# Differential attention: the softmax reciprocal used in place, a shorter output norm, and new operation times in the planner

## The chip, the core and the metric

The kernel runs on one core of a Trainium2 chip. The metric is device time in microseconds (us) of one launch. The core's engines are TensorE (PE; its weight loads are listed as PEld), VectorE (DVE), ScalarE (ACT) and GpSimd (POOL); SyncE (SP) issues the DMAs. Each engine works through its own instructions in their order, and engines wait for each other by semaphores.

## What is computed

One decoder layer: three token mixers (a convolution branch, differential attention, cross-attention into memory), each projected and gated, summed, and projected once more. The change lies in differential attention: 8 heads over 1024 positions, two causal softmax maps each, and an RMS norm of each head's output.

```python
s = einsum(q, k) * scale + bias            # bias = -slope_h * distance, causal
p = softmax(s)                             # two maps, m = 0 and 1
a = p[:, :, 0] - lam * p[:, :, 1]
o = einsum(a, v)
o = rms_norm(o, subln_g) * (1.0 - lambda_init)
o = o * silu(gate) ; y_diff = o @ w_proj
```

## The kernel before

All is float32; matrix products that need precision are split into a high and a low half, three matmuls for one. The kernel has stages. Ahead of attention come the input projections and the convolution. The attention stage comes next, and behind it the last projections (the second half of the attention projection with a GH/GL operand, heads 4 to 7, then the output projection).

**A group of attention** is one head and 256 queries (`g`, two blocks `t` of 128): 32 groups, heads in order, and within a head `g` in the order 2, 3, 0, 1. A group's steps are:

- `pair` (`scores`): for one block and up to 512 keys, four matmuls write two `sc` banks (L1032, L1034). DVE adds the distance bias out of the bank and takes the row maximum (L1038). When a block has all its keys, DVE makes `nm` (L1050), ACT takes the two exponentials with their sums (L1052), DVE makes the reciprocals `rc` (L1054) and a factor (L1055) and combines both maps into one (L1056). POOL copies the first map's reciprocal into a tile `r0` (L1058), since the block's rows are divided by it only in the norm.
- `trans`: PE turns four 128x128 blocks of the combined map into a `tp` bank (L1076), ACT copies it out as `a` (L1078).
- `prod`: PE multiplies `a` with the values into the bank `av` (L1084). After a group's last one, ACT copies `o` out (L1089) and `norm` is issued.
- `norm`: ACT squares `o * r0` with a sum per row (L1098); `rstd_of` makes 1/sqrt from Ln and Exp on ACT (L174, L175) and one Newton step of five POOL operations (L173, L176 to L179); POOL multiplies by `r0` (L1101), DVE scales `o` (L1103).
- `turned`, below called the o-turn: PE turns `o` (L1110), ACT scales it by the norm's gain (L1113), POOL multiplies the gate (L1114), and SP stores it (L1116 for heads 4 to 7).

**Filler.** Projections that need nothing of the running group are cut into steps of six 128x512 matmuls (L78, L79, L80 with operands hH/hL). There are 136 such steps from the first score matmul on; 104 belong to two earlier branches, 32 to the projection of heads 0 to 3, which may start only when the o-turn of head 3's last group is placed.

**What sets the order.** PE's order is written by a planner that runs when the kernel is built. It keeps a clock `now` and lists of the times when DVE, ACT and POOL are busy; `run(eng, start, *costs)` books operations there (each cost times `SLACK`, 1.25, plus `HOP`, 0.3). Of the streams load, prod, trans, pair and o-turn it takes the step that is ready first; when the best one is not ready within `IDLE` (0.4) of `now`, it places a filler step instead, while there are any:

```python
if used < len(fill) and free and best[0] > max(now, fill_at) + IDLE:
    ...
    f()
    used += 1
```

The numbers in `pair_step`, `prod_step`, `trans_step` and so on are this planner's durations in us. They set no time on the chip, but decide which step stands next on PE. The other engines' order is made by a scheduler from the program with PE's order given. What is left of the filler when the streams are empty runs behind the attention stage, while the last o-turns go out to memory and come back as the operand `gin` (L1365) of the next stage.

Of the kernel before, what the change touches and what calls it, by code (L numbers as in the profile page):

```python
# [15 lines left out]
P = 128  # L16
# [14 lines left out]
def hybrid_layer(  # L31
# [36 lines left out]
    def new(pool, shape, tag, dt=F32, bufs=None):  # L68
        return pool.tile(shape, dt, tag=tag, name=tag, bufs=bufs)
# [896 lines left out]
    with ExitStack() as st:  # L966
# [42 lines left out]
        def scores(h, g, T, A):  # L1009

            slope = 2.0 ** -(h + 1)
            A["p"], A["r0"] = [], None
            steps = []
            for t in range(2):
                i = 2 * g + t
                n = P * (i + 1)
                nh = (n + 511) // 512
                R = {}
                for hf in range(nh):
                    def pair(t=t, i=i, n=n, hf=hf, nh=nh, R=R):  # L1020
                        if t == 0 and hf == 0:
                            A["r0"] = new(tiny, [P, 2], "r0", bufs=4)
                        if hf == 0:
                            R["mx"] = new(tiny, [P, 2, 2], "mx")
                            R["p"] = (new(ap_, [P, (2 * g + 2) * P], f"p{g}"), new(ap_, [P, S], "p"))
                        mx, pm = R["mx"], R["p"]
                        k0 = hf * 512
                        w = min(512, n - k0)
                        sc = [mm_bank("sc") for _ in range(2)]
                        q, ts = T["q", i // 4], slice(i % 4 * P, i % 4 * P + P)  # L1030
                        for m in range(2):
                            nc.tensor.matmul(sc[m][:, :w], lhsT=q[:, m, ts], rhs=T["k", hf][:, m, :w],  # L1032
                                             start=True, stop=False)
                            nc.tensor.matmul(sc[m][:, :w], lhsT=q[:, m, ts], rhs=T["kL", hf][:, m, :w],  # L1034
                                             start=False, stop=True)
                        d0 = S - P - P * i + k0
                        for m in range(2):
                            nc.vector.tensor_tensor_reduce(  # L1038
                                out=pm[m][:, k0:k0 + w], in0=sc[m][:, :w], in1=dist[:, d0:d0 + w], scale=1.0,
                                scalar=-3.0e38, op0=ALU.add, op1=ALU.max, accum_out=mx[:, hf, m:m + 1])  # L1040
                        if hf < nh - 1:
                            return
                        p0, p1 = pm
                        nm = new(tiny, [P, 2], "nm")
                        sm = new(tiny, [P, 2], "sm")
                        rc = new(tiny, [P, 2], "rc")
                        c1 = new(tiny, [P, 1], "c1")
                        if nh == 2:
                            nc.vector.tensor_tensor(mx[:, 0, :], mx[:, 0, :], mx[:, 1, :], op=ALU.max)
                        nc.vector.tensor_scalar_mul(nm, mx[:, 0, :], -slope)  # L1050
                        for m in range(2):
                            nc.scalar.activation(pm[m][:, :n], pm[m][:, :n], AF.Exp, bias=nm[:, m:m + 1],  # L1052
                                                 scale=slope, accum_out=sm[:, m:m + 1])
                        nc.vector.reciprocal(rc, sm)  # L1054
                        nc.vector.tensor_scalar(c1, sm[:, 0:1], rc[:, 1:2], nlam[:, 0:1], op0=ALU.mult, op1=ALU.mult)  # L1055
                        nc.vector.scalar_tensor_tensor(p0[:, :n], p1[:, :n], c1[:, 0:1], p0[:, :n],  # L1056
                                                 op0=ALU.mult, op1=ALU.add)
                        nc.gpsimd.tensor_copy(A["r0"][:, t:t + 1], rc[:, 0:1])  # L1058
                        A["p"].append(p0)
                    steps.append(pair)  # L1060
            return steps

# [30 lines left out]

        def norm(A):
            o, ss, y = A["o"], new(tiny, [P, 2], "oss"), new(tiny, [P, 2], "osy")
            junk = new(ap_, [P, P], "ojunk", bufs=1)
            for t in range(2):
                nc.scalar.activation(junk, o[:, t * P:(t + 1) * P], AF.Square, scale=A["r0"][:, t:t + 1],  # L1098
                                     accum_out=ss[:, t:t + 1])
            rstd_of(y, ss, [P, 2], 1.0 / P, 1e-6, eps6, pool=tiny, tags=("onv", "ont"))  # L1100
            nc.gpsimd.tensor_tensor(y, y, A["r0"], op=ALU.mult)  # L1101
            for t in range(2):
                nc.vector.tensor_scalar_mul(o[:, t * P:(t + 1) * P], o[:, t * P:(t + 1) * P], y[:, t:t + 1])  # L1103

        def turned(h, g, A):

# [15 lines left out]
                nc.sync.dma_start(dst[h][:, sl], r2f(src))  # L1122

        ORDER, IDLE = (2, 3, 0, 1), 0.4
        PARTS, SLACK, HOP, CHAIN, LOAD, AB, CHUNK, FIRST = 4, 1.25, 0.3, 8.0, 3.0, 3, 3.0, 11.0

        def bank(W, b, r, c0, half, done, parts):

# [68 lines left out]
        for n, steps in enumerate(todo):  # L1197
            if n == 29:
                held = len(fill)
            fill += [(f, 0.0, False) for at, f in ahead_of if at == n]  # L1200
            (begin, first), *more = steps

            ahead = todo[n + 1][0][0] if n + 1 < len(todo) else lambda: None
            begins[len(fill)] = begin
            steps = [lambda f=first, ahead=ahead: (ahead(), f())] + more
            fill += [(f, UNIT, f is steps[-1]) for f in steps]
# [11 lines left out]
        def run(eng, start, *costs):  # L1218

            for c in costs:  # L1220
                c, q = c * SLACK, busy[eng]
                at = next((i for i in range(len(q)) if q[i][1] > start and max(q[i - 1][1] if i else 0.0, start) + c
                           <= q[i][0]), len(q))
                start = max(q[at - 1][1] if at else 0.0, start)
                q.insert(at, (start, start + c))
                del q[:-40]
                start += c
            return start + HOP
# [5 lines left out]
        def el(n):  # L1234
            return 0.06 + n / 960

        def pair_step(n, h, g, t, hf, f):
            i = 2 * g + t
            w, last_ = min(512, P * (i + 1) - hf * 512), (i + 1) * P <= hf * 512 + 512
            needs = [("cut", h, i // 4), ("cut", h, hf)] + ([("turned", n - 4)] if hf == 0 and n >= 4 else [])  # L1240

            def after(at):
                for m in range(2):
                    x = run("DVE", at - 2 * w / 2400 * (1 - m) + HOP, el(w))
                    slots.append(x)
                    slots.pop(0)
                if last_:
                    t_of["read", h, g] = at
                    w_ = P * (i + 1)
                    x = run("DVE", x, 0.07, 0.07) if hf else run("DVE", x, 0.07)  # L1250
                    x = run("ACT", x, *[0.1 + el(w_)] * 2)
                    x = run("DVE", x, 0.08, 0.19)
                    x = run("DVE", x, el(w_))
                    t_of["p", n, t] = x
            return f, needs, lambda: max(slots[0], now + ahead() - AHEAD), 4 * w / 2400, after

# [12 lines left out]
        def prod_step(n, h, g, jp, c, f):  # L1269
            def after(at):  # L1270
                t_of["used", c] = at
                if jp == g:
                    t_of["av", n] = run("ACT", at + HOP, 0.27)
                    t_of["o", n] = run("DVE", run("ACT", t_of["av", n], 0.17, 0.17) + CHAIN, 0.17, 0.17)
                    t_of["done", h, g] = at
            needs = [("a", c), ("turn", h, jp // 2)] + ([("av", n - 1)] if n else []) + \
                    ([("norm2", n - 4)] if jp == g and n > 3 else [])
            return f, needs, lambda: 0.0, 4 * (384 if jp == g else 512) / 2400, after
# [48 lines left out]
        while any(streams.values()):  # L1327
# [8 lines left out]
            if used < len(fill) and free and best[0] > max(now, fill_at) + IDLE:  # L1336
                now = max(now, fill_at)
                f, cost, end = fill[used]
                with tc.high_priority(offset=0 if cost else -60):
                    f()  # L1340
                used += 1
                now += cost
                parts += cost > 0
                if end:
                    run("DVE", now + HOP, el(512))
                    fill_at = now + CHUNK if parts in chunks else 0.0
                continue
# [89 lines left out]
```

## Time and profile before

| | us |
|---|---|
| median of 3 runs (lowest, highest) | 1762.25 (1761.45, 1763.59) |
| profiled execution | 1759.21 |
| its span | 1757.4 |
| PE busy | 1653.6 |
| DVE, ACT, POOL busy | 1294.1, 919.6, 910.3 |
| attention stage, first score matmul to first matmul on GH | 1212.0 to 1617.0 |

The span is the time from the first to the last instruction of the profiled execution; 1.8 us lie around it. Matmuls are pipelined, so a row's PE time overlaps the next row's: the pace of PE is read from the starts of successive matmuls. A line's idle time is what the engine stood still ahead of it, with the instruction that ended the wait. The granted clock is 1.00 for 2.4 GHz and 0.50 for 1.2 GHz.

### The profile page before, as it was taken

To read this page: it belongs to the slowest core of one execution; us is meant where nothing else is said; L and a number is where in the kernel's file an instruction comes from. 1 tells how busy PE (TensorE), PEld (TensorE's weight loads), DVE (VectorE), ACT (ScalarE), POOL (GpSimd) and SP (SyncE) were. 2 spreads that over 40 slices of the span, in tenths; PEclk is the share of its full clock that TensorE was granted. 3 is DMA by queue.
4 is the path that set the end of the run, shared out by engine and by line. 5 is a ranking of instruction groups with operands and counts; after the bars stand their busy time and mean duration, and the time that the engine had idled before them with its cause. 6 is when DMAs were issued, how large, how long until landed. Compare 5 with 4: busy or idle time off the path is not lost. (4 is left out here: it accounts for less than half of the span.)

```text
span 1757.4 us, 24237 instructions
## 1 busy us (share of the span) xinstructions
PE 1653.6 (94%) x7882; PEld 1369.1 (78%) x7882; DVE 1294.1 (74%) x2170; ACT 919.6 (52%) x1949; POOL 910.3 (52%) x921
## 2 busy tenths in 40 slices
PE   6999999989999999888999999989997999999999
PEld 5788888868787777667888778867786878877787
DVE  7879997998999999675764797744665676675911
ACT  5614635334444445465655786753666776763300
POOL 3320201688765666555665676545547564557820
PEclk8999999999999999999999999999998999999999
DMA  7410212232333345543444233278577455565632
GB/s 273 147 33 19 90 50 76 96 112 86 118 110 95 114 139 162 174 162 120 150 162 151 85 97 121 77 276 253 152 236 259 125 174 159 151 225 189 212 115 90
DMA packets 201399, 247.51 MB, mean 141 GB/s; under 512 B 15377, under 2 KB 109590, under 8 KB 201272
## 3 DMA queue, kind: packets, MB, share of 16 engines
q1 hardware_dynamic: 201272, 245.96, 43.5%
q8 instruction: 62, 1.02, 0.2%
q14 instruction: 65, 0.53, 0.1%
HBM read 172.50 MB, written 73.40 MB: 140 GB/s over the span
## 5 line engine op out<-in xcount | busy, mean ns | idle before, releaser
L422 DVE SCALAR_TENSOR_TENSOR cv<-u,cw,cv 128x512 f32<-128x512 f32 x464 | 349.0, 752 | 9.9
L113 POOL TENSOR_TENSOR wL<-wraw,wH 128x512 fp32r<-128x512 f32 x104 | 143.8, 1398 | 255.2 <-ACT wH L112 162.4
L78 PE MATMUL mm<-hH,wH 128*128 128x512 f32 x512 | 206.8, 404 | 0.6 <-DVE sg L1178 0.6
L79 PE MATMUL mm<-hL,wH 128*128 128x512 f32 x512 | 201.9, 394 | 0.0
L80 PE MATMUL mm<-hH,wL 128*128 128x512 f32 x512 | 201.7, 394 | 0.0
L623 POOL TENSOR_TENSOR wL<-wraw,wH 128x512 fp32r<-128x512 f32 x114 | 169.8, 1490 | 57.5 <-ACT wH L622 56.4
L622 ACT CAST wH<-wraw 128x512 fp32r<-128x512 f32 x190 | 115.6, 615 | 105.5 <-PE tp L640 34.8
L640 PE MATMUL tp<-hH,wH 128*128 128x512 f32 x304 | 122.8, 404 | 32.0 <-ACT sx L645 32.0
L1038 DVE CUSTOM_DVE_ANT_0 p<-sc,dist 128x512 f32<-128x512 f32 (+3 forms) x192 | 100.4, 551 | 59.1 <-PE sc L1034 58.6
L1052 ACT ACTIVATE p<-p,nm 128x768 f32<-128x768 f32 (+7 forms) x128 | 98.3, 770 | 45.1 <-DVE nm L1050 45.0
L640 PE MATMUL tp<-hL,wH 128*128 128x512 f32 x304 | 121.0, 398 | 0.0
L640 PE MATMUL tp<-hH,wL 128*128 128x512 f32 x304 | 120.7, 397 | 0.0
L80 PEld LDWEIGHTS mm<-hH,wL 128*128 128x128 f32 x512 | 97.3, 190 | 21.3
L78 PEld LDWEIGHTS mm<-hH,wH 128*128 128x128 f32 x512 | 97.7, 191 | 18.6 <-DVE sg L1178 0.8
L79 PEld LDWEIGHTS mm<-hL,wH 128*128 128x128 f32 x512 | 97.6, 191 | 17.7
L623 POOL TENSOR_TENSOR wL<-ws,wH 128x512 fp32r<-128x512 f32 x38 | 52.4, 1378 | 113.5 <-ACT wH L622 97.5
L112 ACT CAST wH<-wraw 128x512 fp32r<-128x512 f32 (+1 forms) x112 | 64.4, 589 | 72.2 <-PE mm L80 34.4
L640 PEld LDWEIGHTS tp<-hH,wH 128*128 128x128 f32 x304 | 58.8, 193 | 49.1 <-ACT sx L645 37.1
L645 ACT COPY sx<-tp 128x512 f32<-128x512 f32 x152 | 88.1, 580 | 15.4 <-PE tp L640 10.9
L623 DVE TENSOR_TENSOR wL<-wraw,wH 128x512 fp32r<-128x512 f32 x76 | 72.0, 948 | 19.6 <-ACT wH L622 18.8
L622 ACT CAST wH<-ws 128x512 fp32r<-128x512 f32 x76 | 46.9, 617 | 69.2 <-PE tp L640 61.0
L726 ACT ACTIVATE sx<-sx 128x512 f32<-128x512 f32 x56 | 35.4, 632 | 84.8 <-DVE sx L648 84.3
(315 smaller groups left out, 4857.9 us busy)
## 6 DMA issues: line engine op xcount, KB each, us to landing
wraw<-in_w_in_dram SPq DMA_DIRECT2D x184, 256.0 KB, 3.3
sg<-sgT SPq DMA_DIRECT2D x65, 256.0 KB, 3.2
sgT<-sx SPq DMA_DIRECT2D x48, 256.0 KB, 3.3
qf<-qT SPq DMA_DIRECT2D x32, 256.0 KB, 5.4
kf<-kT SPq DMA_DIRECT2D x32, 256.0 KB, 4.2
yT<-sg SPq DMA_DIRECT2D x32, 256.0 KB, 3.6
w<-cvT SPq DMA_DIRECT2D x22, 256.0 KB, 2.8
mw<-in_w_mem_kv_dram SPq DMA_DIRECT2D x16, 256.0 KB, 6.6
```

The lines of the kernel that those rows point to most:

```text
L78: nc.tensor.matmul(ps, lhsT=lh, rhs=rh, start=start, stop=False)
L79: nc.tensor.matmul(ps, lhsT=lh, rhs=rl, start=False, stop=False)
L80: nc.tensor.matmul(ps, lhsT=ll, rhs=rh, start=False, stop=stop)
L112: self.high(kk)(H[:, :w], raw[:, :w])
L113: self.low(kk).tensor_tensor(L[:, :w], raw[:, :w], r2f(H[:, :w]), op=ALU.subtract)
L422: nc.vector.scalar_tensor_tensor(ps if j < CONV_K - 1 else acc, u[:, at - j:at - j + 512], cw[:, c, 30 - j:31 - j], ps, op0=ALU.mult, op1= ...
L622: nc.scalar.copy(H, a)
L623: (nc.gpsimd if n in (1, 3, 4, 6) else nc.vector).tensor_tensor(L, a, r2f(H), op=ALU.subtract)
L640: nc.tensor.matmul(R[bank], lhsT=l[:, ks], rhs=r, start=start and k == 0 and i == 0, stop=stop and k == 3 and i == 2, skip_group_check=True)
L645: last[0] = nc.scalar.copy(R[n], R[bank])
L1038: nc.vector.tensor_tensor_reduce(out=pm[m][:, k0:k0 + w], in0=sc[m][:, :w], in1=dist[:, d0:d0 + w], scale=1.0, scalar=-3.0e38, op0=ALU.add ...
L1052: nc.scalar.activation(pm[m][:, :n], pm[m][:, :n], AF.Exp, bias=nm[:, m:m + 1], scale=slope, accum_out=sm[:, m:m + 1])
```

## The change

`r0` is no tile any more but a list of the reciprocal's columns, which are kept in ten buffers; the POOL copies go. `norm` is written out: one POOL operation (`onv`, L1100), Ln, Exp and Square on ACT (L1101 to L1103), the Newton step in two fused DVE operations on 128x2 (L1104, L1105), and the factor `r0` as a second scalar of the last scaling on DVE (L1108). In the planner DVE's small operations are longer, the constant `CHAIN` (8.0 us for the norm) is replaced by booked operations, and a filler weight load books its ACT and POOL work.

```diff
-                            A["r0"] = new(tiny, [P, 2], "r0", bufs=4)
+                            A["r0"] = []
-                        rc = new(tiny, [P, 2], "rc")
+                        rc = new(tiny, [P, 2], "rc", bufs=10)
-                        nc.gpsimd.tensor_copy(A["r0"][:, t:t + 1], rc[:, 0:1])
+                        A["r0"].append(rc[:, 0:1])
...
-            rstd_of(y, ss, [P, 2], 1.0 / P, 1e-6, eps6, pool=tiny, tags=("onv", "ont"))
-            nc.gpsimd.tensor_tensor(y, y, A["r0"], op=ALU.mult)
+            nc.gpsimd.tensor_scalar(v, ss, 1.0 / P, 1e-6, op0=ALU.mult, op1=ALU.add)
+            nc.scalar.activation(x, ss, AF.Ln, bias=eps6[:, 0:1], scale=1.0 / P)
+            nc.scalar.activation(y, x, AF.Exp, scale=-0.5)
+            nc.scalar.activation(x, y, AF.Square)
+            nc.vector.scalar_tensor_tensor(x, x, -0.5, v, op0=ALU.mult, op1=ALU.mult)
+            nc.vector.scalar_tensor_tensor(y, x, 1.5, y, op0=ALU.add, op1=ALU.mult)
             for t in range(2):
-                nc.vector.tensor_scalar_mul(o[:, t * P:(t + 1) * P], o[:, t * P:(t + 1) * P], y[:, t:t + 1])
+                nc.vector.tensor_scalar(o[:, sl], o[:, sl], y[:, t:t + 1], A["r0"][t], op0=ALU.mult, op1=ALU.mult)
...
-                    x = run("DVE", x, 0.07, 0.07) if hf else run("DVE", x, 0.07)
+                    x = run("DVE", x, 0.3, 0.4) if hf else run("DVE", x, 0.4)
                     x = run("ACT", x, *[0.1 + el(w_)] * 2)
-                    x = run("DVE", x, 0.08, 0.19)
-                    x = run("DVE", x, el(w_))
+                    x = run("DVE", x, 0.16, 0.27, 0.3 + w_ / 800)
...
-                    t_of["o", n] = run("DVE", run("ACT", t_of["av", n], 0.17, 0.17) + CHAIN, 0.17, 0.17)
+                    x = run("ACT", run("ACT", t_of["av", n], 0.49, 0.49), 0.2, 0.2, 0.2)
+                    t_of["o", n] = run("DVE", x, 0.15, 0.15, 0.45, 0.45)
...
-            fill += [(f, 0.0, False) for at, f in ahead_of if at == n]
+            fill += [(f, 0.0, len(f.ks) if isinstance(f, Weights) else 0) for at, f in ahead_of if at == n]
...
+                if not cost:
+                    for _ in range(end):
+                        run("POOL", run("ACT", now + LOAD, 0.52), 1.3)
+                    end = False
```

On POOL, the norm of one group in the last third of the stage stood like this before (`onv` to `osy`, with one copy of a reciprocal among it):

```order
L173 TENSOR_SCALAR onv<-oss 128x2
L1058 COPY r_14490<-rc 128x1
L176 TENSOR_TENSOR ont<-osy 128x2
L177 TENSOR_TENSOR ont<-ont,onv 128x2
L178 TENSOR_SCALAR ont<-ont 128x2
L179 TENSOR_TENSOR osy<-osy,ont 128x2
L1101 TENSOR_TENSOR osy<-osy,r_14144 128x2
```

On POOL in the same third of the stage now:

```order
L113 TENSOR_TENSOR wL<-wraw,wH 128x512
L999 TENSOR_TENSOR kL<-kf,k 128x512 x2
L999 TENSOR_TENSOR q<-qf,q 64x512 x2
L1100 TENSOR_SCALAR onv<-oss 128x2 x2
L1119 TENSOR_TENSOR oT<-oT,gd 128x256 x2
```

Of seven POOL operations one is left; the Newton step now stands on DVE as L1104 and L1105, ahead of the two scalings L1108.

On PE, the last o-turn of the stage before (operands hH/hL are filler):

```order
L78 MATMUL mm<-hH_99,wH 128x512
L79 MATMUL mm<-hL_101,wH 128x512
L80 MATMUL mm<-hH_99,wL 128x512
L1110 MATMUL tp<-ident,o 128x128 x2
L78 MATMUL mm<-hH_99,wH 128x512
L79 MATMUL mm<-hL_101,wH 128x512
L80 MATMUL mm<-hH_99,wL 128x512
```

On PE, the last two o-turns now (GH/GL is the operand that comes back from memory):

```order
L1076 MATMUL tp<-ident,p_15707 128x128
L1076 MATMUL tp<-ident,p_15764 128x128 x2
L1115 MATMUL tp<-ident,o 128x128 x2
L1084 MATMUL av<-v,a 128x128 x7
L1115 MATMUL tp<-ident,o 128x128 x2
L78 MATMUL mm<-GH,wH 128x512
L79 MATMUL mm<-GL,wH 128x512
L80 MATMUL mm<-GH,wL 128x512
```

The filler that stood around the last o-turns has moved to earlier places; none stands there now. The last filler matmul of the stage now stands here, in head 5, with a score pair behind it:

```order
L78 MATMUL mm<-hH_99,wH 128x512
L79 MATMUL mm<-hL_101,wH 128x512
L80 MATMUL mm<-hH_99,wL 128x512
L1032 MATMUL sc<-k,q 128x256
L1034 MATMUL sc<-kL,q 128x256
```

Between that place and the last o-turn PE's order now holds attention's steps alone.

## Rows read from the trace of the kernel before

**Rows 1.** The page's part 1: busy time, share of span, instructions

```profile
PE 1653.6 (94%) x7882; PEld 1369.1 (78%) x7882; DVE 1294.1 (74%) x2170; ACT 919.6 (52%) x1949; POOL 910.3 (52%) x921
```

**Rows 2.** Windows: length, PE, PEld, DVE, ACT, POOL busy (count), granted clock, DMA

```profile
1330.00:1340.00 10.00, 7.47 (x34) 5.46 (x33) 8.70 (x23) 7.55 (x20) 9.68 (x9) 0.96 1.05 393
1340.00:1350.00 10.00, 2.79 (x9) 2.30 (x9) 3.60 (x9) 2.72 (x10) 7.61 (x16) 0.50 1.06 312
...
1480.00:1490.00 10.00, 8.05 (x43) 6.34 (x42) 6.77 (x25) 5.37 (x17) 3.21 (x5) 1.00 0.82 211
...
1530.00:1540.00 10.00, 10.00 (x72) 9.17 (x71) 5.38 (x20) 7.48 (x23) 3.49 (x5) 1.00 0.68 212
...
sum 400.00, PE 374.40 PEld 321.99 DVE 263.16 ACT 261.91 POOL 231.69; mean PE 9.36 PEld 8.05 DVE 6.58 ACT 6.55 POOL 5.79
```

**Rows 3.** The same in windows of 20 us: the one with most DVE

```profile
1320.00:1340.00 20.00, 17.47 (x98) 14.45 (x96) 15.83 (x43) 15.43 (x37) 15.80 (x17) 0.98 0.81 296
```

**Rows 4.** Waits of PE, 1200 to 1610: us, times, longest

```profile
PE sc L1032 <- DVE mx L1038: 9.8, 9, 2.2
PE tp L1110 <- DVE o L1103: 9.1, 2, 7.2
```

**Rows 5.** Timeline of the longest wait: start, us, engine, line [idle before]

```profile
1346.58 0.20 POOL L1101 TENSOR_TENSOR osy<-osy,r 128x2 f32<-128x2 f32 x1
...
1346.81 0.48 DVE L1103 TENSOR_SCALAR o<-o,osy 128x128 f32<-128x128 f32 x2 [3.06 <-POOL osy L1101]
...
1347.24 0.66 PE L1110 MATMUL tp<-ident,o 128*128 128x128 f32 x2 [7.21 <-DVE o L1103]
```

**Rows 6.** DVE's lines, 1210 to 1610: busy, mean ns | idle before

```profile
L1038 DVE CUSTOM_DVE_ANT_0 p<-sc,dist 128x512 f32<-128x512 f32 (+3 forms) x192 | 100.4, 551 | 59.1 <-PE sc L1034 58.6 <-issue 0.3
L1056 DVE SCALAR_TENSOR_TENSOR p<-p,c,p 128x640 f32<-128x640 f32 (+3 forms) x64 | 63.1, 986 | 1.3
L1103 DVE TENSOR_SCALAR o<-o,osy 128x128 f32<-128x128 f32 x64 | 25.4, 438 | 16.7 <-POOL osy L1101 16.6
L1050 DVE TENSOR_SCALAR nm<-mx 128x2 f32<-128x2 f32 x64 | 25.2, 393 | 1.5
L1149 DVE TENSOR_TENSOR sg<-mm,sg 128x512 f32<-128x512 f32 x27 | 18.5, 687 | 12.7 <-PE mm L80 12.6
L1055 DVE TENSOR_SCALAR c<-sm,rc,nlam 128x1 f32<-128x1 f32 x64 | 17.3, 271 | 1.3
L1038 DVE DVE_READ_ACCUMULATOR2_ANT mx<- 128x1 f32 x192 | 15.7, 82 | 0.0
L1054 DVE RECIPROCAL rc<-sm 128x2 f32<-128x2 f32 x64 | 10.4, 162 | 31.1 <-ACT p L1052 29.4 <-ACT ont L174 0.8 <-POOL kL L999 0.3
L1049 DVE TENSOR_TENSOR mx<-mx 128x2 f32<-128x2 f32 x32 | 9.8, 306 | 0.8
L1178 DVE TENSOR_TENSOR sg<-mm,sg 128x512 f32<-128x512 f32 x13 | 9.0, 689 | 14.5 <-PE mm L80 10.4 <-DMA sg<-sgT 4.1
```

**Rows 7.** Timeline of PE: two successive 512-column matmuls, and a run of products

```profile
1332.58 0.40 PE L78 MATMUL mm<-hH,wH 128*128 128x512 f32 x1
1332.81 0.40 PE L79 MATMUL mm<-hL,wH 128*128 128x512 f32 x1
...
1575.40 2.84 PE L1084 MATMUL av<-v,a 128*128 128x128 f32 x24
```

**Rows 8.** Timeline of the last group's norm on ACT and DVE

```profile
1591.09 0.37 ACT L1089 COPY o<-av 128x256 f32<-128x256 f32 x1 [2.31 <-PE av L1084]
...
1596.55 0.93 DVE L1103 TENSOR_SCALAR o<-o,osy 128x128 f32<-128x128 f32 x2 [1.79 <-POOL osy L1101]
```

**Rows 9.** Timeline of PE behind the last o-turn

```profile
1602.29 0.38 PE L1110 MATMUL tp<-ident,o 128*128 128x128 f32 x2
...
1616.97 0.39 PE L78 MATMUL mm<-GH,wH 128*128 128x512 f32 x1
...
1620.26 0.50 PE L79 MATMUL mm<-GL,wH 128*128 128x512 f32 x1 [0.85 <-DVE GL L84]
```

More of the change, by code (lines that the diff above doesn't have):

```diff
@@ L1095, in norm @@
             o, ss, y = A["o"], new(tiny, [P, 2], "oss"), new(tiny, [P, 2], "osy")
+            v, x = new(tiny, [P, 2], "onv"), new(tiny, [P, 2], "ont")
             junk = new(ap_, [P, P], "ojunk", bufs=1)
             for t in range(2):
-                nc.scalar.activation(junk, o[:, t * P:(t + 1) * P], AF.Square, scale=A["r0"][:, t:t + 1],
-                                     accum_out=ss[:, t:t + 1])
-            rstd_of(y, ss, [P, 2], 1.0 / P, 1e-6, eps6, pool=tiny, tags=("onv", "ont"))
-            nc.gpsimd.tensor_tensor(y, y, A["r0"], op=ALU.mult)
+                nc.scalar.activation(junk, o[:, t * P:(t + 1) * P], AF.Square, scale=A["r0"][t], accum_out=ss[:, t:t + 1])
+            nc.gpsimd.tensor_scalar(v, ss, 1.0 / P, 1e-6, op0=ALU.mult, op1=ALU.add)
[4 more added lines that the diff above has]
+            nc.vector.scalar_tensor_tensor(y, x, 1.5, y, op0=ALU.add, op1=ALU.mult)
             for t in range(2):
-                nc.vector.tensor_scalar_mul(o[:, t * P:(t + 1) * P], o[:, t * P:(t + 1) * P], y[:, t:t + 1])
+                sl = slice(t * P, t * P + P)
+                nc.vector.tensor_scalar(o[:, sl], o[:, sl], y[:, t:t + 1], A["r0"][t], op0=ALU.mult, op1=ALU.mult)
         def turned(h, g, A):
@@ L1124, in hybrid_layer @@
         ORDER, IDLE = (2, 3, 0, 1), 0.4
-        PARTS, SLACK, HOP, CHAIN, LOAD, AB, CHUNK, FIRST = 4, 1.25, 0.3, 8.0, 3.0, 3, 3.0, 11.0
+        PARTS, SLACK, HOP, LOAD, AB, CHUNK, FIRST = 4, 1.25, 0.3, 3.0, 3, 3.0, 11.0
         def bank(W, b, r, c0, half, done, parts):
```

## The prediction

> **What bounds the kernel now.** I read the page's busy shares first: PE is busy for 1653.6 of 1757.4 us [rows 1], so a change that leaves PE's work as it is can only move the time that PE stands still or runs at the lower clock. PE's work is the same before and after: the orders hold the same matmuls, line by line, and up to the first score matmul in the same sequence. All that moves lies in the attention stage and just behind it.
>
> Then the windows of that stage: of 400 us PE is busy for 374.4 [rows 2]. Its pace comes from successive starts: 0.23 us for a 512-column matmul (1332.58 to 1332.81), 0.118 us for each of the 24 records of L1084, of which two make a product, so 0.24 [rows 7]. With these, and 0.17, 0.13 and 0.11 us for 384, 256 and 128 columns (estimates from the first number by columns and from the second for small ones), the stage's PE work is: 136 filler steps of six at 0.23 = 188 us; scores 71; turns of maps, values and outputs 46; products 70. Sum 375 us. From the first score matmul at 1212.0 to the first on GH at 1617.0 [rows 9] the stage takes 405 us. It **loses 30 us** to standing and to the lower clock, and that is all that could be gained.
>
> Who makes PE wait is in its waits: 9.8 us for a free score bank and 9.1 us for a scaled `o` ahead of the o-turn, 7.2 of these at one place [rows 4]. That place shows what the new norm is aimed at: `osy` leaves POOL at 1346.8, DVE scales, and PE starts 7.21 us late [rows 5], in a window where the granted clock has fallen to 0.50 [rows 2].
>
> **The change part by part.**
>
> The norm. Five POOL operations, the POOL product and 64 POOL copies go; one ACT Square and two fused DVE operations of 128x2 come. POOL is busy for 232 of 400 us here [rows 2], so its freed time is worth nothing by itself; the gain is that the chain no longer queues on POOL behind 512-column work. The last norm took 5.5 us from the copy of `o` to the start of the scaling, 6.4 us to its end [rows 8]. The two new DVE operations are not in the trace: by the two other 128x2 operations with one source they cost 0.16 to 0.39 us [rows 6]; I take 0.16, that of the reciprocal, since L1050 stands behind an accumulator read, and its 0.39 may hold a wait for it. 64 of these in the stage are 10 us of DVE time, beside PE. The extra scalar in L1108 I cost at nothing, with up to 0.1 us each as the other end; it is the same pass over 128 columns. DVE is no bound while filler stands beside it (263 of 400 us), so the added time is hidden there. The `rc` buffers remove a wait of DVE for POOL's copy and add none: ten columns cover the groups in flight.
>
> PE's order. This is the large part. With longer DVE times and no 8 us reserve, the planner finds itself waiting more often and **spends its filler sooner**, while it sets o-turns nearer to their products. Counted in the orders: before, 126 of 136 filler steps stand ahead of the last o-turn and 10 behind it, and the longest run without one is 8.7 us of PE work. After, all 136 are spent in head 5. There follow 58 us of PE work without filler (26 score blocks of 512, 10 of 384, 10 of 256, 8 of 128 columns: 20 us; 97 products: 23; 131 turns: 15), then at once the matmuls on GH. A second bare run of 17 us stands in heads 3 and 4, where the filler that may start is spent and the rest is still locked.
>
> What is DVE's work in the 58 us? 54 of 192 score reads, 19 of 64 map combinations and 11 of 32 norms stand in DVE's order there. From rows 6: 54/192 of (100.4 + 15.7) = 32.7; 19/64 of (63.1 + 25.2 + 17.3 + 10.4) = 34.4; 8/32 of 9.8 = 2.5; 22/64 of 25.4 = 8.7; 22 new ones at 0.16 = 3.5. Sum 82. Rows overlap a little: the lines of rows 6 add up to 295, and DVE was busy for 263 [rows 2], so times 0.89: **73 us of DVE against 58 us of PE**. So DVE, not PE, sets this stretch. It cannot be busy throughout, since ACT's exponentials stand between its own steps: the densest 20 us before held 15.83 us of DVE, 79% [rows 3], the mean of the stage was 66% [rows 2]. 73/0.79 = 92; at 66% 111; at 100% 73. At the end come about 5 us of the last norm with nothing to do for DVE beside it (rows 8 gives 5.5 with the old chain). I take 92 + 5 = 97, because no filler takes DVE's time there: a **loss of 39 us** (15 to 58).
>
> The 17 us run, by the same count, holds 27 us of DVE lines, 24 by the same factor; with 0.79, 30 us. Part of it can be made up by neighbours with filler: loss 8 us (4 to 14).
>
> Behind the last o-turn. Before, from it to the matmul that waits for the operand of the last head, 18.0 us passed (1602.29 to 1620.26), of which filler covered 14.7 (up to 1616.97) [rows 9]. Now nothing stands there. SP issues its loads in order behind the last store, so the first operand is late too. I take a loss of 13 us (8 with memory less busy, 18 with none of it hidden); before, 0.85 us of standing were left [rows 9].
>
> The rest of the stage, 300 us of PE work with filler between: at the old rate it would lose 24 us (30 x 300/375). The 9.1 us of o-turn waits and the low clock behind them should mostly go, though o-turns now mostly stand only 2 to 12 us of PE work behind their products, before 10.6 to 25. I take 12 us (4 to 25).
>
> Sum: 8 + 39 + 13 + 12 = 72 us lost, less the 30 of before: +42 on the profiled execution's 1759.2, 1801 us. That execution lies 3.0 us under the median of 1762.25, so 1804 on the scale of the runs. With all low ends (4 + 15 + 8 + 4 - 30 = +1) 1763; with all high ends (14 + 58 + 18 + 25 - 30 = +85) 1847.
>
> The clock in the bare stretch. In the trace, a 10 us window with PE busy for 7.47 was followed by one at 0.50, and one with 8.05 kept 1.00 [rows 2]. 58 of 97 us is 60% busy, so the lower level is likely there at times. The Trainium skill, "TensorE: Matmul & The Clock Gate", section "A second HAM failure mode: psum-queue depth-cycling", says that small idle gaps between groups of matmuls make the clock go back and forth and that throughput suffers. By the row alone the sum stays as it is, if DVE is the bound in any case; by the page's rule it becomes the second rival below.
>
> **The rivals.**
>
> Faster than before. In the trace, short runs with little filler hardly cost anything: 1530 to 1540 had PE busy for all 10 us, with DVE at 5.38 [rows 2], because PE worked off maps that DVE had made earlier. If that held for the long run, it would lose 3 us, the short one 2, the tail 8 and the rest 6: 19 against 30, so 1751. It decides once both bare runs together cost under some 10 us. Against it: the stock of maps is two buffers a size, and over two heads DVE must do its 73 us inside the run. 4%.
>
> The clock falls for the whole bare run. PE's 58 us become up to 116, plus 5: loss 63 there, 16 behind; 8 + 63 + 16 + 12 - 30 = +69, 1831. For it: 60% busy. Against: at half the clock PE would be busy nearly throughout, and busy windows have 1.00 [rows 2]. 20%.
>
> The norm does not get shorter. `onv` is still on POOL, in line behind the filler's 512-column subtractions, and DVE now waits for it ahead of its score reads, at 0.16 us work each time; before, DVE waited 16.6 us for POOL here [rows 6]. Then the rest loses its high end, 25: +55, 1817. 10%.
>
> The gains just pay for the bare runs, low ends everywhere: within 0.2%, 5%.
>
> **How the numbers follow.** 0.2% is 3.5 us, about what measuring can tell from no change. My forecast, 1785 to 1820 with DVE as bound, has 55%; a milder loss (1766 to 1785) 6%; the clock 20%; the norm 10%; no change 5%; faster 4%. Faster 0.04, same 0.05, slower 0.91. The range leaves out faster, no change and part of the mild case below (1774), and the far end of the clock case above (1843).
>
> **What would show it.** In the profile after: PE's busy share under 70% in the last 90 to 100 us of attention, with waits of PE for DVE's score reads, for the combined maps and for ACT's copies; DVE at 75 to 80% there; a clock under 1.00 at times; 8 us or more of PE standing ahead of the first matmuls on GH; the norm from `o` copied to scaled in about 4 us, no POOL copies; and the 7.2 us wait gone. I am wrong if PE stays over 85% busy in that stretch, or if the stage from first score matmul to first GH matmul takes less than 410 us.

## The result, and the profile after

The changed kernel takes 1844.56 us (median of 4 runs, 1843.45 to 1846.01) against 1761.87 us before (4 runs): a ratio of 1.0468 with a 95% interval from 1.045 to 1.0486. The direction was forecast; the size was not. The forecast was +42 us and 1804, with a range up to 1843; the measured change is +83 us, and the profiled executions' spans differ by 86.8.

The page's part 1 of the kernel after answers to [rows 1]:

```profile
span 1844.2 us, 24074 instructions
PE 1688.9 (92%) x7882; PEld 1392.1 (75%) x7882; DVE 1318.1 (71%) x2234; ACT 929.5 (50%) x1981; POOL 849.8 (46%) x697
```

PE has the same 7882 records and is busy for 35 us more, with the mean granted clock down from 0.977 to 0.961; the remaining 52 us it stands. Five stretches of the kernel after, by its own fillers: from the first score matmul to the short bare run, that run, filler again, the long bare run up to the last o-turn, and the way out. The columns are those of [rows 2].

```profile
1217.00:1448.00 231.00, 214.36 (x1144) 181.98 (x1143) 138.66 (x384) 127.66 (x322) 95.96 (x93) 0.96 0.61 192
1448.00:1484.00 36.00, 20.42 (x127) 17.16 (x126) 21.76 (x70) 21.62 (x66) 10.08 (x13) 0.82 0.31 98
1484.00:1580.00 96.00, 92.91 (x488) 78.59 (x488) 65.59 (x149) 50.74 (x121) 54.47 (x49) 0.98 0.65 208
1580.00:1698.00 118.00, 79.03 (x434) 66.27 (x432) 71.70 (x242) 73.62 (x216) 29.08 (x37) 0.82 0.16 49
1698.00:1717.00 19.00, 12.32 (x34) 7.89 (x35) 9.31 (x13) 5.81 (x10) 6.76 (x5) 0.68 0.79 270
```

The fourth line is the heart of it. In the long bare run DVE is busy for 71.7 us, as counted from [rows 6] (73). But the run takes 118 us: DVE is busy for 61% of it, where the forecast took 79%. ACT is busy for 73.6 us, no less than DVE. PE's 58 us of work show as 79 us of busy time at a granted clock of 0.82.

The waits of PE in the attention stage of the kernel after (us, times, longest), which answer to [rows 4]:

```profile
PE tp L1115 <- DVE o L1108: 45.8, 15, 7.7
PE av L1084 <- ACT a L1078: 9.1, 8, 1.7
PE tp L1076 <- DVE p L1056: 8.8, 4, 3.2
PE mm L78 <- ACT GH L83: 6.6, 3, 5.4
PE sc L1032 <- DVE mx L1038: 5.9, 14, 1.8
```

The o-turn's wait, 9.1 us in two places before, is 45.8 us in fifteen. The same rows cut by stretch: 10.1 us of o-turn waits up to 1460, 12.5 in the short bare run, 2.4 in the filler after it, 20.9 in the long one. There PE stands for 39 us in all (118 less 79), so o-turns are a good half; ACT's copies of `a` (7.6), the combined maps (6.9) and the score banks (3.1) make up the rest.

Such a wait in full, from the timeline of the kernel after (start, us, engine, line [idle before]), in the long bare run, for the group whose `o` was copied at 1589.89. The first line is its last product, the PE line of 1592.75 the next group's.

```profile
1588.92 0.94 PE L1084 MATMUL av<-v,a 128*128 128x128 f32 x6
...
1589.89 0.37 ACT L1089 COPY o<-av 128x256 f32<-128x256 f32 x1 [1.02 <-PE av L1084]
...
1591.37 0.39 ACT L1099 ACTIVATE ojunk<-o,rc 128x128 f32<-128x128 f32 x1
...
1592.59 1.05 ACT L993 CAST k<-kf 128x1024 fp32r<-128x1024 f32 x1
...
1592.75 0.94 PE L1084 MATMUL av<-v,a 128*128 128x128 f32 x6 [1.20 <-ACT a L1078]
...
1593.54 1.05 ACT L993 CAST q<-qf 128x1024 fp32r<-128x1024 f32 x1
...
1594.48 0.41 ACT L1099 ACTIVATE ojunk<-o,rc 128x128 f32<-128x128 f32 x1
...
1596.29 2.93 POOL L999 TENSOR_TENSOR q<-qf,q 64x512 fp32r<-64x512 f32 x2
...
1596.54 0.30 ACT L1101 ACTIVATE ont<-oss,eps 128x2 f32<-128x2 f32 x1
...
1599.31 0.46 POOL L1100 TENSOR_SCALAR onv<-oss 128x2 f32<-128x2 f32 x2
1599.54 0.43 DVE L1104 SCALAR_TENSOR_TENSOR ont<-ont,onv 128x2 f32<-128x2 f32 x2 [1.43 <-POOL onv L1100]
...
1600.61 0.73 PE L1115 MATMUL tp<-ident,o 128*128 128x128 f32 x2 [6.92 <-DVE o L1108]
```

The norm's own operations take some 3 us. It lasts over 10, since between its two squares stand copies and the two casts of the next head on ACT, ahead of its Ln two exponentials, and ahead of its one POOL operation the next head's subtractions. PE has only some 2.4 us of work between the product and the o-turn in its order (turns, one score pair, the next group's product), and stands for 6.92 us; with PE stand the next scores, and so DVE.

### The profile page after: what moved, and what is told of

The parts are those of the page before. It is cut to its first block, busy times and chain, and to the rows that moved or that the text cites. A ratio compares the mean times of both kernels' runs of the same rounds, so it can differ in the third digit from the quotient of the medians.

```text
span 1844.2 us, 24074 instructions
## 1 busy us (share of the span) xinstructions
PE 1688.9 (92%) x7882; PEld 1392.1 (75%) x7882; DVE 1318.1 (71%) x2234; ACT 929.5 (50%) x1981; POOL 849.8 (46%) x697
## 5 line engine op out<-in xcount | busy, mean ns | idle before, releaser
L113 POOL TENSOR_TENSOR wL<-wraw,wH 128x512 fp32r<-128x512 f32 x104 | 141.4, 1376 | 267.8 <-ACT wH L112 162.3
L623 POOL TENSOR_TENSOR wL<-wraw,wH 128x512 fp32r<-128x512 f32 x114 | 168.4, 1478 | 61.8 <-ACT wH L622 60.9
L1038 DVE CUSTOM_DVE_ANT_0 p<-sc,dist 128x512 f32<-128x512 f32 (+2 forms) x192 | 101.2, 552 | 62.4 <-PE sc L1034 61.4
L1119 POOL TENSOR_TENSOR oT<-oT,gd 128x256 f32<-128x256 f32 x32 | 24.2, 757 | 136.8 <-ACT oT L1118 122.0
L1084 PE MATMUL av<-v,a 128*128 128x128 f32 x576 | 78.5, 292 | 9.1 <-ACT a L1078 9.1
```

What stands on the lines that cost most here:

```text
L113: self.low(kk).tensor_tensor(L[:, :w], raw[:, :w], r2f(H[:, :w]), op=ALU.subtract)
L623: (nc.gpsimd if n in (1, 3, 4, 6) else nc.vector).tensor_tensor(L, a, r2f(H), op=ALU.subtract)
L1038: nc.vector.tensor_tensor_reduce(out=pm[m][:, k0:k0 + w], in0=sc[m][:, :w], in1=dist[:, d0:d0 + w], scale=1.0, scalar=-3.0e38, op0=ALU.add ...
L1084: nc.tensor.matmul(A["av"][:, t * P:t * P + P], lhsT=A["a", jp][:, c * P:c * P + P], rhs=T["v", j // 4][:, j % 4, :], start=j == 0 and t = ...
```

## The experiments

The first four take the change apart. Theory A says that PE's order costs the time (filler spent early, o-turns close behind their products), theory B that the new operations do, theory C that DVE's capacity in the bare runs does. Ratios are to runs of the kernel before in the same series.

**The new operations alone.** The changed kernel with the planner's old numbers; PE's order is that of before.

```diff
-                    x = run("DVE", x, 0.3, 0.4) if hf else run("DVE", x, 0.4)
+                    x = run("DVE", x, 0.07, 0.07) if hf else run("DVE", x, 0.07)
...
-                    x = run("DVE", x, 0.16, 0.27, 0.3 + w_ / 800)
+                    x = run("DVE", x, 0.08, 0.19)
+                    x = run("DVE", x, el(w_))
...
-                    x = run("ACT", run("ACT", t_of["av", n], 0.49, 0.49), 0.2, 0.2, 0.2)
-                    t_of["o", n] = run("DVE", x, 0.15, 0.15, 0.45, 0.45)
+                    t_of["o", n] = run("DVE", run("ACT", t_of["av", n], 0.17, 0.17) + 8.0, 0.17, 0.17)
...
-                    for _ in range(end):
-                        run("POOL", run("ACT", now + LOAD, 0.52), 1.3)
```

> The new norm and the reciprocal in place, with the planner's old numbers, so PE's order as before. Theory A (place: the loss comes from the order, which spends the filler early and sets o-turns close to their products): within 1750 to 1764 us, since only part of the 9.1 us of o-turn waits of before can go. Theory B (operations: the longer path over ACT and DVE with POOL's onv in front costs the time): 1790 us or more. Theory C (DVE's capacity in the bare runs): 1755 to 1764 us, there is no bare run in this order.

Measured 1757.36 us against 1759.61: 0.998 (0.9963 to 0.9998). Theory B is out: the operations alone are, if anything, 0.2% faster, with 2.6 us of o-turn waits left of 9.1. PE's waits in its stage:

```profile
PE sc L1032 <- DVE mx L1038: 12.3, 8, 5.3
...
PE tp L1115 <- DVE o L1108: 2.6, 2, 1.7
```

**The new numbers alone.** Old norm, old copies, new planner numbers; PE's order is that of after. Two of the places, against the kernel after:

```diff
...
-                        A["r0"].append(rc[:, 0:1])
+                        nc.gpsimd.tensor_copy(A["r0"][:, t:t + 1], rc[:, 0:1])
...
+            rstd_of(y, ss, [P, 2], 1.0 / P, 1e-6, eps6, pool=tiny, tags=("onv", "ont"))
+            nc.gpsimd.tensor_tensor(y, y, A["r0"], op=ALU.mult)
...
```

> The old norm and the POOL copies, with the planner's new numbers, so PE's order as after. Theory A: 1845 to 1875 us, the old norm is longer and the o-turns are as close. Theory B: about 1762 us. Theory C: 1835 to 1845 us, as after with some 10 us less DVE work.

Measured 1853.3 us, 1.054 (1.0508 to 1.0571). The whole loss, and a little more, comes with the order. With the same order the old norm makes PE wait longer at the o-turns:

```profile
PE tp L1110 <- DVE o L1103: 63.2, 13, 9.0
```

So the shorter norm is worth 9 us in this order by the times and 13 by the ratios (1.054 and 1.0468), and 2 to 4 us in the old one.

**Without the norm.** The changed kernel with `norm(A)` left out.

```diff
                     nc.scalar.copy(A["o"], A["av"][:, :256])
-                    norm(A)
```

> The changed kernel with the output norm left out (o is copied, then turned), PE's order as after. Theory A: the 45.8 us in which PE stood at o-turns go, and with them the clock they cost; 1780 to 1800 us. Theory C: the bare runs lose only the norm's share of DVE, some 12 of 73 us; 1825 to 1835 us.

Measured 1790.33 us (two runs), 1.0172 (1.013 to 1.0214): 54 us less than with it. The long bare run falls from 118 to 98 us (the first line, columns of [rows 2]). The waits move to the next step, the combined maps:

```profile
1538.90:1636.80 97.90, 73.04 (x434) 60.47 (x432) 63.17 (x198) 56.79 (x138) 27.50 (x26) 0.90 0.19 60
...
PE tp L1076 <- DVE p L1056: 19.0, 9, 3.3
PE av L1084 <- ACT a L1078: 8.6, 8, 1.7
```

Theory A's figure. But 98 us for the same 58 of PE work is still far from PE's pace. The run parts waiting from work only in part, since with the norm 17 us of ACT's and 9 of DVE's busy time leave the long bare run too.

**Less DVE work.** The combination of the maps cut to 128 columns.

```diff
-    nc.vector.scalar_tensor_tensor(p0[:, :n], p1[:, :n], c1[:, 0:1], p0[:, :n],
+    nc.vector.scalar_tensor_tensor(p0[:, :P], p1[:, :P], c1[:, 0:1], p0[:, :P],
```

> The changed kernel with the combination of the two maps cut to 128 columns (the rest of the map is left as it is), PE's order as after; it takes some 36 of 63 us off DVE in the stage, about 10 of them in the long bare run. Theory A: o-turn waits stay, 1835 to 1842 us. Theory C: the bare runs shorten by what DVE saves over its density there, 13 to 17 us, and the short one by 4; 1822 to 1828 us.

Measured 1832.53 us, 1.0412 (1.0376 to 1.0448), between the two forecasts. The long bare run took 109 us for 118:

```profile
1573.20:1682.00 108.80, 76.09 (x435) 62.53 (x433) 61.14 (x240) 72.41 (x214) 27.79 (x36) 0.84 0.17 53
```

The 10 us taken off DVE came off it nearly one for one, no more. Were DVE's capacity the bound, its density would have stayed and 13 to 17 us gone; it fell from 61 to 56%. DVE's work lies in line with the rest. ACT's capacity, the like rival, is not the bound alone either: its 72.4 us are those of the changed kernel (73.6), and the run is 9 us shorter.

The next four ask **which of the new numbers** does it. The forecasts set close o-turns (A1) against bare length (A2). All have the new operations; the first three keep the planner's old numbers but for one.

**The norm's booking alone.** The diff of the first experiment without its three lines on `t_of["o", n]`.

> Of the planner's new numbers only the norm's: its path booked on ACT and DVE in place of the 8 us constant; pair times and weight loads as before; new operations. All filler is spent ahead of the last o-turn, the last 20 us of PE work are bare, and half of the o-turns stand under 8.2 us behind their product (4 under 4 us). Theory A1 (close o-turns cost most): 1775 to 1795. Theory A2 (what costs is the length of the bare run, at the measured 1 us lost for 1 us of PE work): 20 + 6 for the way out, 1775 to 1785; the o-turn waits of PE decide between them: A1 over 15 us of them, A2 under 8.

Measured 1806.94 us, 1.0255 (1.0225 to 1.0285), more than either said. Its waits hold 37.4 us at o-turns, 14 of them:

```profile
PE tp L1115 <- DVE o L1108: 37.4, 14, 7.3
```

Up to its last filler matmul the stage loses 47 us (402 us for 355 of PE work; before, 30 for the whole stage). The bare run behind it takes 43 us for 20 of PE work. Close o-turns cost where filler is near, too; the reading is that too little of it stands between product and o-turn.

**The pair times alone.** The diff of the first experiment without its lines on the pair.

> Of the planner's new numbers only DVE's pair times; the 8 us constant stays; new operations. All filler is spent, the last 40 us of PE work are bare, but the median o-turn stands 13 us behind its product. Theory A1: 1762 to 1775, few o-turns to wait for. Theory A2: 40 us lost and 6 for the way out, 1790 to 1805.

Measured 1793.99 us, 1.0181 (1.0137 to 1.0225). That is A2's range. O-turn waits are 9.1 us, as before the change. The loss lies in the bare run: 71 us for 40 of PE work.

```profile
1208.00:1569.00 361.00, 339.72 (x1886) 290.19 (x1885) 235.56 (x678) 219.21 (x570) 174.96 (x169) 0.98 0.63 195
1569.00:1640.00 71.00, 49.71 (x299) 41.70 (x298) 49.55 (x165) 50.42 (x152) 17.83 (x23) 0.87 0.12 38
```

**The weight loads alone.** The old numbers with the booking of weight loads.

> Of the planner's new numbers only the weight loads that it books; new operations. 129 of 136 filler steps ahead of the last o-turn, no bare run over 9 us. Both theories: as with the old numbers, 1752 to 1765.

Measured 1763.87 us, 1.0013 (0.9997 to 1.0028): nothing.

**The changed kernel with 8 us more for the norm.**

```diff
-                    t_of["o", n] = run("DVE", x, 0.15, 0.15, 0.45, 0.45)
+                    t_of["o", n] = run("DVE", x, 0.15, 0.15, 0.45, 0.45) + 8.0
```

> The changed kernel with 8 us more for the norm in the planner: bare runs of 23 and 47 us of PE work (16.6 and 58 in the changed kernel), but the median o-turn stands 14.6 us behind its product and two under 4 us. Theory A1: the o-turn waits go to under 15 us, 1795 to 1810. Theory A2: the bare runs sum to 71 in place of 75 us, 1835 to 1845.

Measured 1818.54 us, 1.0321 (1.0291 to 1.0351), between both. The o-turn waits fell to 9.5 us as A1 said, but the bare run of 47 us still took 92: the waits reappear at the combined maps (15.0 us) and ACT's copies (13.1). So there are two losses: close o-turns, and bare runs, which lost from 0.6 to 1.2 us for each us of PE work over these runs, whatever PE waited for in them.

**POOL out of the norm, in the changed kernel.** `onv` on DVE.

```diff
-            nc.gpsimd.tensor_scalar(v, ss, 1.0 / P, 1e-6, op0=ALU.mult, op1=ALU.add)
+            nc.vector.tensor_scalar(v, ss, 1.0 / P, 1e-6, op0=ALU.mult, op1=ALU.add)
```

> The changed kernel with the norm's first operation (onv) on DVE in place of POOL, where it stands in line behind 512-column subtractions; PE's order as after. If POOL's line makes PE wait at the o-turns, a third or more of the 45.8 us goes: 1815 to 1830 us. If ACT's line does (squares, Ln, Exp and Square stand behind exponentials and casts): 1838 to 1848 us.

Measured 1851.1 us (two runs), 1.0535 (1.0496 to 1.0575), a little above the range named for ACT's line; o-turn waits 44.0 us. POOL's line, which ended the wait in the timeline above, is not what holds the norm on the whole. ACT's remains as the likely one: in the changed kernel's attention stage DVE's first operation of the norm (L1104) waited 19.8 us for ACT and 2.3 for POOL. No run took ACT's line away.

**Filler spread over the stage.**

```diff
-            free = used < held or ("norm2", 4 * HD - 1) in t_of
+            free = (used < held or ("norm2", 4 * HD - 1) in t_of) and used < 30 + 4.0 * sum(e[0] == "norm2" for e in t_of)
```

> The changed kernel with a filler allowance that grows by 4 steps with each placed o-turn (30 to begin with), so that filler lasts to the end: 117 of 136 steps ahead of the last o-turn, six bare runs of 12 to 14 us of PE work in place of 17 and 58; o-turns as close as after (median 6 us, five under 4). If bare runs cost in proportion to their sum (79 us here, 75 after): 1835 to 1850 us. If it is the long one that costs, because maps and scores made ahead carry PE over a short one: 1785 to 1810 us.

Measured 1868.31 us, 1.0633 (1.0596 to 1.067), worse than my worst figure. The six bare runs of 12 to 14 us of PE work together, and the stage up to the last o-turn:

```profile
sum 134.30, PE 98.24 PEld 86.17 DVE 87.84 ACT 81.64 POOL 31.46; mean PE 16.37 PEld 14.36 DVE 14.64 ACT 13.61 POOL 5.24
...
1211.00:1692.80 481.80, 387.44 (x2073) 328.56 (x2071) 281.38 (x833) 268.00 (x713) 167.23 (x173) 0.90 0.44 143
```

They lose some 57 us over their 77 us of PE work, less than the changed kernel's two (79 us over 75). The loss has moved. From the first score matmul to the last o-turn pass 482 us for some 349 of PE work (375 less the 19 filler steps left behind), so by this estimate the rest of the stage loses some 76 us, where it lost 27 in the changed kernel. So bare runs are not what makes this order the worst. Two waits grew: o-turns 49.8 us, combined maps 25.8. Filler left over behind the last o-turn does not help.

**Two tries for a faster kernel.** Seven us in place of eight for the norm in the planner (`+ 7.0` in the first experiment's diff), and the first experiment with `onv` on DVE.

> The new operations with the planner's old numbers, but 7 us in place of 8 for the norm: median o-turn 13.6 us behind its product, the least 7.4, no bare run over 9 us, 17 filler steps left behind the last o-turn (10 before). If the shorter norm can be used by nearer o-turns without standing: 1748 to 1757 us. If o-turns at 7 us already wait for the norm, whose measured length goes up to 13 us: 1760 to 1772 us.

> The new operations and the planner's old numbers, with onv on DVE, so that POOL has no part in the norm. PE's order as before. With o-turns at 10.6 us and more the norm's end hardly matters: 1753 to 1760 us, as with onv on POOL; if POOL's line was behind the last o-turn waits of that kernel (2.6 us), up to 3 us less.

Measured 1754.9 us, 0.998 (0.9956 to 1.0003), and 1755.45 us, 0.9989 (0.9969 to 1.0008). Neither can be told from the first experiment or, by its interval, from before.

**The clock in the long bare run.** Throw-away turns on PE where the planner sees PE idle without filler: six at a time in the first run (below), three in the second.

```diff
+            while best[0] > now + IDLE:
+                warm = mm_bank()
+                for b in range(6):
+                    nc.tensor.transpose(warm[:, b % 4 * P:b % 4 * P + P], ident, ident)
+                now += 0.68
             now = max(now, best[0])
```

> The changed kernel with throw-away turns of a constant (six of 128 columns, read by nobody) put on PE wherever the planner sees PE idle and has no filler: the bare runs stay as long, but PE stands less. If a part of the long bare run's 60 us loss is the lower clock (about 20 us by PE's busy time there, 79 us for 58 us of work), that part comes back: 1820 to 1832 us. If the steps' latencies on DVE and ACT alone set the run and the clock only fills standing time: 1838 to 1850 us.

Measured 1863.4 us, 1.0594 (1.0554 to 1.0634): neither. The 864 turns were more than PE had room for: the long bare run took 140 us, with PE busy for 132 of it.

> As the run with six throw-away turns, which filled the long bare run with more than PE had room for (PE busy throughout at 1.00, the run 140 us in place of 118), but with three, some 37 us of PE work there. If the lower clock is a part of its own of the 60 us loss: the clock is 1.00 there, the run takes 98 to 108 us, the kernel 1825 to 1836 us. If the clock only fills time in which PE would stand: the clock is 1.00 and the run still takes 115 to 122 us, the kernel 1840 to 1850 us.

Measured 1847.99 us, 1.0497 (1.0467 to 1.0527). Four windows of the long bare run, with the columns of [rows 2]:

```profile
1620.00:1640.00 20.00, 16.04 (x127) 14.71 (x126) 14.03 (x43) 11.44 (x27) 6.70 (x7) 1.00 0.09 27
1640.00:1660.00 20.00, 17.91 (x145) 16.63 (x143) 13.57 (x50) 13.55 (x42) 1.12 (x3) 1.00 0.05 14
1660.00:1680.00 20.00, 17.47 (x139) 15.95 (x137) 12.39 (x42) 13.29 (x38) 3.30 (x5) 1.00 0.09 27
1680.00:1700.00 20.00, 18.89 (x161) 17.91 (x159) 9.68 (x40) 13.39 (x45) 2.04 (x5) 1.00 0.11 35
```

The clock is 1.00 from 1620 on (0.91 and 0.83 in the two windows ahead), and the run takes 122 us, 118 without the turns. In the changed kernel the same windows have 0.88, 0.74, 0.83 and 0.82. So the full clock brought nothing that its own price (the turns on PE) left to be seen. The reading that the lower clock fills time in which PE would stand anyway fits, and is not shown by itself: the o-turn waits fell to 26.2 us, and the turns may only have taken their place.

## Why the prediction was right in direction and wrong in size

The cause that it names is shown: PE's work is the same, the new order spends all filler in head 5, and what follows is bare. The new operations alone were forecast at next to nothing and measured at -0.2%; the order alone gives +5.4%. What it says of the bare runs' pace and of the o-turns is not right, and so three of four terms were too small. In the profiled executions:

| term | forecast (range) | measured |
|---|---|---|
| long bare run, loss over PE's work | 39 (15 to 58) | 118 - 58 = 60 |
| short bare run | 8 (4 to 14) | 35.1 - 16.6 = 18.5 |
| rest of the stage | 12 (4 to 25) | 21.8 + 4.8 = 27 |
| way out | 13 (8 to 18) | 5.8 up to the first matmul on GH |
| less the loss of before | -30 | -30 |
| sum | +42 | +81 |

The remaining 5.6 us of the spans' 86.8 lie ahead of the first score matmul (1212.0 and 1217.6), where PE's order is the same. Over the experiments this start lies between 1207.7 and 1217.6, so I put it to the executions, not to the change.

**The step that failed** is "So DVE, not PE, sets this stretch", with the density that I gave DVE in the bare runs for it. The 73 us of DVE work were right (71.7). I divided by the densest 20 us of before [rows 3], "because no filler takes DVE's time there". But that window had filler on PE, which the planner had set where a step was not ready: while PE works on filler, DVE and ACT can go ahead with what was set before. Without filler, as I read it, each step of a group waits for the one ahead, through three in-order engines, and PE waits with them. The mean of the stage, 66% [rows 2], which I had as the other end, gives 111 + 5 = 116; 118 were measured, but that is luck, since 66% is a density beside filler. The runs speak for latency and against DVE's capacity: DVE is 61% busy, work taken off it lowers that to 56% and comes off the run one for one, and taking the norm out takes off 20 us, after which PE waits for the combined maps. Of the prediction's signs, PE under 70% came in the long run (79 of 118 us, 67%), DVE at 75 to 80% did not. The same wrong density made the short run too cheap.

**The rest of the stage** was sized by the thought that a shorter norm lets o-turns stand closer. I had the distances, "2 to 12 us of PE work behind their products", and did not set them against the norm's length. That was 4.3 to 21.1 us before, from the copy of `o` to its scaling's end, with a median of 7.0; after, it is 3.3 to 13.3, with a median of 5.7. An o-turn that stands nearer than its own norm is long is mostly a wait of PE: o-turn waits, which "should mostly go", are 12.5 of the 27 us. The booking of the norm alone costs 2.5%, the largest single number.

**The rivals.** "The norm does not get shorter" was near the truth in mechanism (median 5.7 us where I said about 4; with the old order 7.7), and its 25 us for the rest of the stage were near the 27, but not for its reason: POOL's `onv` moved to DVE made nothing faster. The clock as a bound of its own is not borne out by the two runs with throw-away turns, though its time (1831) was nearer than mine. The window at 0.50 that stands behind it [rows 2] is also the one in which PE stood for the 7.21 us of [rows 5].

**The way out** cost 5.8 us up to the first matmul on GH. The forecast's stretch was longer, to the matmul that waits for the last head's operand: before, the eleventh on GH, at 1620.26. After, that one starts at 1710.01:

```profile
1697.02 0.66 PE L1115 MATMUL tp<-ident,o 128*128 128x128 f32 x2 [3.25 <-DVE o L1108]
1703.06 0.79 PE L78 MATMUL mm<-GH,wH 128*128 128x512 f32 x1 [5.38 <-ACT GH L83]
...
1710.01 0.79 PE L79 MATMUL mm<-GL,wH 128*128 128x512 f32 x1 [0.22 <-DVE GL L84]
```

These 13.0 us hold some 2.5 us of PE work, so by its own measure this term was 10.5 us and inside its range. It does not show in the sum, since from the eleventh matmul to the end the kernel after takes 134.2 us and the kernel before 137.1; why is open.

**Terms put low.** DVE's new operations of 128x2 took 0.32 and 0.37 us on the mean, not 0.16:

```profile
L1105 DVE SCALAR_TENSOR_TENSOR osy<-ont,osy 128x2 f32<-128x2 f32 x32 | 11.7, 367 | 0.8
L1104 DVE SCALAR_TENSOR_TENSOR ont<-ont,onv 128x2 f32<-128x2 f32 x32 | 10.3, 321 | 22.3 <-ACT ont L1103 19.8 <-POOL onv L1100 2.3
```

That is 22 us of DVE time for 10 forecast, without effect beside filler. Their median is 0.16, as forecast; the last section shows what lifts the mean. The second scalar of L1108, put at nothing, costs 0.06 us each by the medians (345 ns for 283).

What the experiments leave open: how the two losses share the changed kernel's 110 us exactly, since each alone (+2.5%, +1.8%) moves the other, and why the stretches beside filler lost so much more when the filler was spread.

## What to carry to other kernels

A planner that places filler whenever it sees a wait spends it sooner the longer its model's times are; where the filler is finite, better single durations can give a worse order. Count in the new order where the filler ends and how far each consumer stands behind its producer, and set that distance against the longest measured latency, queues included, not against the sum of the operations. For a stretch without independent work, do not take the density of the densest window, which had filler to thank for it: DVE was busy for 55 to 70% of the long bare runs here (20 us of PE work or more behind the last filler, no throw-away turns).

## What was not expected of the hardware

The granted clock of 0.67 to 0.93 in the bare run looked like a cost of some 20 us (79 us of PE busy time for 58 of work; by the mean clock alone an estimated 13, since 58/0.82 is 71). With throw-away work it went to 1.00 and the run did not get shorter (122 us for 118): the 20 us can't be read as a gain that waits to be taken.

Small DVE operations were held beside POOL's. Of the 64 new ones of 128x2, 49 took 0.14 to 0.16 us. The other 15 took 0.39 to 1.26 us, and each ran beside a POOL operation and ended within 0.03 us of its end:

```profile
L1105 DVE SCALAR_TENSOR_TENSOR osy<-ont,osy x32: 150/161/1262, 1254.9 to 1696.3; 128x2 f32<-128x2 f32 x32
...
1286.52 0.73 POOL L1125 TENSOR_TENSOR oT<-oT,gd 128x256 fp32r<-128x256 f32 x1 [0.25 <-ACT gd L1124]
1286.64 0.63 DVE L1104 SCALAR_TENSOR_TENSOR ont<-ont,onv 128x2 f32<-128x2 f32 x1 [4.16 <-ACT ont L1103]
```

(The first line gives the shortest, median and longest of L1105 in ns.) The same holds for the 18 of 64 of L1050 that took over 0.25 us before the change. So its mean of 0.39 us is not the wait for an accumulator read that the prediction thought possible. No operation of L1050, L1104 and L1105 that started while one of POOL's ran ended before it in the kernel after; all 64 reciprocals (L1054), 20 of them beside POOL, took 0.15 to 0.17 us. The prediction had its 0.16 from the reciprocal, which was not held. Why is not shown by a run of its own.
